# Banded attention in a hybrid layer kernel: the splitting and masking of a pair's probabilities issued in one group behind its turns

## The chip, the cores and the metric

The kernel runs on one core of a Trainium2 chip. The metric is the device time of one execution in microseconds. Five engines with queues of their own take part: TensorE (PE in the profile, with its weight loads as PEld), VectorE (DVE), ScalarE (ACT), GpSimd (POOL) and SyncE (SP, which here only issues DMAs). Each engine works its queue strictly in the order in which the program was written, and semaphores make an instruction wait for another engine.

## The reference

One decoder layer over 2048 positions and 1024 channels. A normalised and modulated input goes through one projection into two groups of heads: 8 heads of forgetting attention, and 8 query heads (2 key heads) of attention in a sliding window of 128 with sinks. Both outputs are gated, concatenated and projected back. What the change touches is the window attention:

```python
s = einsum('bnqhgd,bnshd->bnhgqs', qb, kk) * d ** -0.5     # a block of 128 queries, its own and the previous 128 keys
mask = (rel >= 0) & (rel < WINDOW) & valid_blk              # the band
s = where(mask, s, -inf)
p = softmax(concatenate([s, sink], -1), -1)[..., :-1]       # the sink is one more column of the softmax
out = einsum('bnhgqs,bnshd->bnqhgd', p, vv)
```

## The kernel before

**The window attention is done in 32 pairs.** A `Pair` is two neighbouring blocks of 128 queries for two heads, so four 128x128 tiles. Its steps, with the engine and the line:

- `scores` (PE, L871): 12 products in 16-bit halves into the PSUM tile `pss`, of which there is one.
- `maxima` (DVE): L879 folds the band of the previous key block into the own one, so that each row keeps 128 columns; L881 writes the sink into one more column; L884 takes the maxima; L886 makes the bias `b_nb` of 4 numbers a row from them.
- `exps` (ACT, L893): four exponentials of 128x129 into `sm_`, with their sums.
- `turn` (PE, L900): four transposes of `sm_` into the PSUM tile `pxb`. Then its two parts, which are not issued on the spot but registered with `after`: the **high part** (ACT, L914) rounds `pxb` to 16 bits into `fold[:, 0]`; the **low part** (DVE, L905) subtracts that from `pxb` into `fold[:, 1]`; a reciprocal of the sums (DVE, L907); and four **selections** on POOL (L909 and L911 for the high part, then both again for the low part), which write the two triangles of the band into `ptb`, zero elsewhere.
- `pv` (PE, L924): 24 products (18 for the first block) of `ptb` with the values into `pob`, and DVE's L930, which scales by the reciprocal into `on`. Two of eight pairs store `on` from the POOL queue at once (L274), the others after being split in two (L284, L280, L281).

`fold`, `ptb`, `sm_`, `pss` and `pxb` have one buffer each.

**Between these steps stand the projections.** `punits` is a list of units of TensorE work (3 products of 512 columns at L339, or 12 of 128 at L357), which make the queries, values and gates that are needed later. Their results leave PSUM through ACT and DVE (L731, L736, L383, L379, L362, L366), through three banks. Loading and splitting the projections' weights hangs on the same list: ACT's L256 makes the high part of a weight, DVE's L262 the low part, and POOL issues their loads (L216) and the small DMAs L225 and L230.

**What sets the order.** The order is written out by hand. `after(n, f)` puts `f` on a list, and `tick()` runs what is due. One round of the loop over the pairs is: `tick`, the maxima of the pair, a quarter of the units, `tick`, its exponentials, a quarter, `tick`, a quarter, `tick`, a quarter, then `pv` of the pair before, `turn` of this pair, `scores` of the next. So what a turn registers with `after(1, ...)` is issued at the head of the next round, in front of the next pair's maxima; what it registers with `after(2, ...)` is issued a quarter of a round later, behind the next pair's maxima and in front of its exponentials.

Of the kernel before, what the change touches and what calls it, by code (L numbers as in the profile page):

```python
# [15 lines left out]
AF = mybir.ActivationFunctionType  # L16
# [27 lines left out]
def hybrid_layer(  # L44
# [17 lines left out]
    V, A, G, PE, SP = nc.vector, nc.scalar, nc.gpsimd, nc.tensor, nc.sync  # L62
# [20 lines left out]
    def sm(n, tag):  # L83
        return small.tile([P, n], F32, tag=tag, name=tag)
# [112 lines left out]
    def after(n, f):  # L197
        late.append([n, f])
# [219 lines left out]
    def turn(ci, k):  # L418

        px = ps_x.tile([P, CH], F32, tag="x", name="px")  # L420
        for u in range(4):
            PE.transpose(px[:, u * P:(u + 1) * P], xt[ci * 4 + u][:, k * P:(k + 1) * P], ident[:])
        hf = hst.tile([P, CH], F32, tag="hf", name="hf")
        hi, lo = hT[ci][:, 0, k, :], hT[ci][:, 1, k, :]

        def scaled():
            for dst in ([hi] if k % 2 == 0 else []) + [hf[:]]:
                A.activation(dst, px[:], AF.Identity, scale=Gp[:, k:k + 1], bias=Shp[:, k:k + 1])

        def split():  # L430
            if k % 2:
                V.tensor_copy(hi, hf[:])
            V.tensor_tensor(lo, hf[:], hi, op=ALU.subtract)

        return scaled, split

    def turn_x(ci, k):
        scaled, split = turn(ci, k)
        after(1, scaled)
        after(2, split)  # L440
# [12 lines left out]
    with tc.manual_schedule():  # L453
# [172 lines left out]
        w_low("kb", 0, 1)  # L626
        w_low("vb", 0, 1)
        turned = [turn(0, k) for k in range(5)]
        squares(1)
        shf0 = col8("shf0")  # L630
# [22 lines left out]
        for k in range(KT):  # L653
            turned[k][0]()
            turned[k][1]()
            if k >= 2:
                next(root1, None)
            if k + 5 < KT:
                turned.append(turn(0, k + 5))
# [195 lines left out]
    class Pair:  # L855
# [40 lines left out]
        def turn(self):  # L896

            px = ps_t.tile([P, 4, P], F32, tag="t", name="pxb")
            for n in range(4):
                PE.transpose(px[:, n, :], self.sm_[:, n, 1:P + 1], ident[:])  # L900
            self.ptt = ptp.tile([P, 2, 2, 4, P], F16, tag="pt", name="ptb")
            fold = ptp.tile([P, 2, 4, P], F16, tag="fo", name="fold")

            def low():
                V.tensor_tensor(fold[:, 1], px[:], fold[:, 0], op=ALU.subtract)  # L905
                self.rinv = sm(4, "b_ri")
                V.reciprocal(self.rinv[:], self.rs[:])  # L907
                for n in range(2):
                    G.affine_select(self.ptt[:, 0, n], fold[:, n], [[0, 4], [-1, P]], ALU.is_ge, 0.0,  # L909
                                    base=-1, channel_multiplier=1)  # L910
                    G.affine_select(self.ptt[:, 1, n], fold[:, n], [[0, 4], [1, P]], ALU.is_ge, 0.0,  # L911
                                    base=0, channel_multiplier=-1)

            after(1, lambda: A.activation(fold[:, 0], px[:], AF.Copy))  # L914
            after(2, low)

        def pv(self):
            j, i = self.j, self.i
# [810 lines left out]
```

## Time and profile before

| | |
|---|---|
| median of 3 runs | 1174.29 us (1173.09 to 1176.38) |
| the profiled execution's own time | 1176.95 us |
| its span in the profile | 1175.2 us |
| DVE, ACT, POOL busy over the span | 80%, 56%, 16% |
| the pairs' part of the span | 149.0 us (first scores) to 431.1 us (last value products) |
| selections | 128, 91.4 us of POOL's 192.6 us |
| low parts | 32, 21.9 us of VectorE |

The rows of a timeline read: start in us, length in us, engine, line, operation, output and inputs by the program's names, partitions and size, count; in brackets the time for which the engine stood idle before, and the instruction on another engine that ended the wait. A group's row has the count, the busy sum and the mean in ns of one, and then the idle time before its instructions with those who ended it.

### The profile page before, as it was taken

The page shows a single profiled execution, that of the slowest core. Times are in us where ns is not written, and L with a number is a line of the kernel's source. Part 1 is how long each engine was busy: PE and PEld are TensorE (multiplying, and loading weights), DVE is VectorE, ACT ScalarE, POOL GpSimd, SP SyncE. Part 2 cuts the span into 40 slices and gives each one's busy share as a digit, 9 for nine tenths or more (in the row PEclk, how much of TensorE's full clock was granted, in tenths as well). Part 3 has the DMA queues.
Part 4 walks back from the last instruction along what each step waited for, and adds up shares of the span by engine and source line. Part 5 has one row for each costly group of instructions (what it writes and reads, how often), then busy time and mean ns, then how long its engine had stood idle before and what let it go on. Part 6 is the DMA issues. An engine that isn't in the chain of part 4 may idle for free.

```text
span 1175.2 us, 26821 instructions
## 1 busy us (share of the span) xinstructions
PE 1127.3 (96%) x10637; PEld 671.1 (57%) x10637; DVE 935.1 (80%) x2167; ACT 662.0 (56%) x1150; POOL 192.6 (16%) x293
## 2 busy tenths in 40 slices
PE   5899999999899999999999999999999999999997
PEld 2465555755457986555555555555556555544444
DVE  7876668688786757788888999888897897778885
ACT  2784445454554531476766767666776788543332
POOL 1000135535445531001000100001000000000000
PEclk9899999999999999999999999999999999999999
DMA  9745433414324323513425422223311237586743
GB/s 332 280 124 87 78 93 73 91 51 106 90 65 89 73 43 75 81 47 95 74 66 60 111 43 74 61 44 73 52 33 47 68 86 231 137 213 199 195 144 108
DMA packets 123481, 120.19 MB, mean 102 GB/s; under 512 B 64948, under 2 KB 100828, under 8 KB 123356
## 3 DMA queue, kind: packets, MB, share of 16 engines
q1 hardware_dynamic: 112088, 85.69, 27.0%
q0 software_dynamic: 10832, 32.50, 13.8%
q8 instruction: 83, 1.36, 0.6%
q14 instruction: 42, 0.34, 0.1%
q10 hardware_dynamic: 436, 0.28, 0.1%
HBM read 64.75 MB, written 25.18 MB: 77 GB/s over the span
## 4 chain that ended last, share of the span: by engine, by line
PE 71%; DVE 11%; issue 8%; DMA 5%; ACT 2%; POOL 2%; SPq 0%; DVEq 0%; ACTq 0%; POOLq 0%
PE bk L339 24%; PE bk L1522 13%; PE bk L357 7%; PE sta L1311 4%; PE sta L1310 4%; PE bk L1261 4%; PE poa L1336 3%; PE poa L1337 3%; PE poa L1334 3%; DMA wa<-in_w_ada_dram 2%; PE pob L924 2%; PE pss L871 1%; DVE a_m L1264 1%; DVE pha L1324 1%; PE pxb L900 1%
## 5 line engine op out<-in xcount | busy, mean ns | idle before, releaser
L1317 ACT ACTIVATE p<-sta,lift,scl_qk 128x1024 f32<-128x1024 f32 (+2 forms) x160 | 171.8, 1074 | 131.8 <-PE sta L1311 82.7
L339 PE MATMUL bk<-hT,wh_qk 128*128 128x512 f16 x768 | 194.7, 378 | 0.0
L1324 DVE TENSOR_TENSOR pha<-p,pha 128x1024 f16<-128x1024 f32 (+2 forms) x160 | 169.0, 1056 | 0.2 <-ACT pha L1321 0.2
L1264 DVE TENSOR_REDUCE a_m<-bk 128x1 f32<-128x512 f32 x192 | 130.3, 685 | 46.8 <-PE bk L1261 45.8
L1522 PE MATMUL bk<-wohl,oz 128*128 128x512 f16 x744 | 165.3, 379 | 1.0 <-DVE oz L1471 0.7
L1321 ACT ACTIVATE pha<-p 128x1024 f16<-128x1024 f32 (+2 forms) x160 | 148.1, 926 | 5.9 <-PE poa L1337 1.2
L1522 PEld LDWEIGHTS <-oz 128*128 128x128 f16 x744 | 71.8, 99 | 82.8 <-DVE oz L1471 1.8
L1337 PE MATMUL poa<-vt,pha 128*128 128x65 f16 x1088 | 116.1, 192 | 1.4 <-DVE pha L1324 1.4
L1334 PE MATMUL poa<-vt,pha 128*128 128x65 f16 x1088 | 116.6, 193 | 0.8 <-DVE ona L1343 0.7
L1336 PE MATMUL poa<-vt,pha 128*128 128x64 f16 x1088 | 116.6, 194 | 0.0
L339 PEld LDWEIGHTS <-wh_qk 128*128 128x128 f16 x768 | 72.2, 97 | 74.4 <-issue 1.9
L1310 PE MATMUL sta<-T 128*128 128x512 f16 (+1 forms) x320 | 110.9, 346 | 2.8 <-ACT p L1317 2.7
L1261 PE MATMUL bk<-T 66*128 66x512 f16 (+2 forms) x320 | 109.7, 348 | 3.2 <-DVE a_m L1264 1.9
L1334 PEld LDWEIGHTS <-pha 128*128 128x128 f16 x1088 | 101.5, 96 | 15.5 <-DVE ona L1343 1.9
L1311 PE MATMUL sta<-T 69*128 69x512 f16 (+1 forms) x320 | 109.8, 348 | 0.0
L1336 PEld LDWEIGHTS <-pha 128*128 128x128 f16 x1088 | 100.9, 97 | 11.4
L1337 PEld LDWEIGHTS <-pha 128*128 128x128 f16 x1088 | 100.8, 99 | 1.8 <-DVE pha L1324 1.8
L339 PE MATMUL bk<-hT,wh_za 128*128 128x512 f16 x384 | 99.7, 378 | 0.0
L357 PE MATMUL bk<-wh_va,hT 128*128 128x128 f16 x1536 | 89.9, 219 | 0.0
L357 PEld LDWEIGHTS <-hT 128*128 128x128 f16 x1536 | 87.1, 98 | 4.1 <-issue 2.1
L339 PE MATMUL bk<-hT,wh_zb 128*128 128x512 f16 x384 | 89.0, 380 | 0.0
L339 PE MATMUL bk<-hT,wh_qb 128*128 128x512 f16 x384 | 87.4, 379 | 0.0
(447 smaller groups left out, 1917.7 us busy)
## 6 DMA issues: line engine op xcount, KB each, us to landing
hT<-in_x_dram SPq DMA_DIRECT2D x20, 512.0 KB
wa<-in_w_ada_dram SPq DMA_DIRECT2D x16, 512.0 KB
z_d<-tz POOLq DMA_DIRECT2D x32, 256.0 KB, 3.0
T<-stq SPq DMA_DIRECT2D x64, 128.0 KB
T<-z_d SPq DMA_DIRECT2D x16, 512.0 KB
out_dram<-hT SPq DMA_DIRECT2D x15, 512.0 KB
xt<-in_x_dram SPq DMA_DIRECT2D x12, 512.0 KB
qs<-qf SPq DMA_DIRECT2D x80, 64.0 KB
```

Of the source, the lines that this page charges most:

```text
L339: PE.matmul(ps, whl[:, a, k, :], hT[ci][:, b, k, :], start=(k == 0 and n == 0), stop=(k == KT - 1 and n == 2))
L357: PE.matmul(ps[:, u * P:(u + 1) * P], hT[ci][:, a, k, u * P:(u + 1) * P], whl[:, b, k, :], start=(k == 0 and n == 0), stop=(k == KT - 1 an ...
L1261: PE.matmul(mx[:, :w], T[0:XM, 0, i * P:(i + 1) * P], T[0:XM, 2, pc * CH:pc * CH + w], start=True, stop=True)
L1310: PE.matmul(self.st[:, o:o + w], T[:, 3, kb_], T[:, 1, qc], start=True, stop=False)
L1311: PE.matmul(self.st[:, o:o + w], T[0:XR, 2, kb_], T[0:XR, 0, qc], start=False, stop=not diag)
L1317: A.activation(self.p32[:, :self.w], self.st[:, :self.w], AF.Exp, scale=scl[f"qk{self.hd}"][:], bias=lift[:])
L1321: A.activation(self.ph[:, 0, :self.w], self.p32[:, :self.w], AF.Copy)
L1324: V.tensor_tensor(self.ph[:, 1, :self.w], self.p32[:, :self.w], self.ph[:, 0, :self.w], op=ALU.subtract)
L1334: PE.matmul(po[:, u, :], ph[:, 0, pq], vt[:, b, hd, 0:65], start=(self.first and n == 0 and u == 0), stop=False)
L1336: PE.matmul(po[:, u, 0:64], ph[:, 0, pq], vt[:, b, hd, 65:VW], start=False, stop=False)
L1337: PE.matmul(po[:, u, :], ph[:, 1, pq], vt[:, b, hd, 0:65], start=False, stop=(self.last and n == len(self.blocks) - 1))
L1522: PE.matmul(py, self.hl[:, i, k, :], w_slot(8 * j + k)[:, cc], start=(k == 0 and m_ == 0), stop=(k == KT - 1 and m_ == 2))
```

## The change

The low part, the reciprocal and the four selections are issued at the first tick behind the turn instead of the second, together with the high part:

```diff
-            def low():
+            def split():
+                A.activation(fold[:, 0], px[:], AF.Copy)
                 V.tensor_tensor(fold[:, 1], px[:], fold[:, 0], op=ALU.subtract)
                 self.rinv = sm(4, "b_ri")
                 V.reciprocal(self.rinv[:], self.rs[:])
...
                     G.affine_select(self.ptt[:, 1, n], fold[:, n], [[0, 4], [1, P]], ALU.is_ge, 0.0,
                                     base=0, channel_multiplier=-1)
 
-            after(1, lambda: A.activation(fold[:, 0], px[:], AF.Copy))
-            after(2, low)
+            after(1, split)
```

The instructions, their sizes and their counts stay as they are, and so does the order on PE, ACT and SP. Lines from L905 on move by one or more: the high part is L905 in the changed kernel, the low part L906, the reciprocal L908, the selections L910 and L912.

On VectorE, at the pair whose turns run at 200.4 us of the profile, the difference reads (rows with + are the changed kernel's; `fold` is the split pair, `pss` the next pair's scores):

```order
 L930 TENSOR_TENSOR on<-pob,b_ri 128x256
+L906 TENSOR_TENSOR fold<-pxb,fold 128x512
+L908 RECIPROCAL b_ri<-b_rs 128x4
 L879 COPY_PREDICATED pss<-dmask,pss 128x2x2x128
 L881 COPY pss<-snd_qb_1543 128x2x2
 L884 TENSOR_REDUCE b_m<-pss 128x4
 L886 TENSOR_SCALAR b_nb<-b_m,nscl_qb_1541 128x4
-L905 TENSOR_TENSOR fold<-pxb,fold 128x512
-L907 RECIPROCAL b_ri<-b_rs 128x4
 L740 TENSOR_TENSOR stb<-qc,stb 128x512
```

The low part and the reciprocal move from behind the maxima's four instructions to in front of them; where VectorE had work of a projection between the maxima and the low part, they move past that too.

On POOL, at the selections of the pair whose turns run at 165.7 us, the rows of the kernel before (`o_d` and `z_d` are DRAM tensors, `tz` a gate projection that VectorE finishes after the maxima):

```order
L274 DMA o_d_69<-on 128x2x128
L381 DMA z_d<-tz 128x512
L909 AFFINE_SELECT ptb<-fold 128x512
L911 AFFINE_SELECT ptb<-fold 128x512
L909 AFFINE_SELECT ptb<-fold 128x512
L911 AFFINE_SELECT ptb<-fold 128x512
L225 DMA mx_d_74<-w_mx 128x1
```

and those of the changed kernel:

```order
L274 DMA o_d_69<-on 128x2x128
L910 AFFINE_SELECT ptb<-fold 128x512
L912 AFFINE_SELECT ptb<-fold 128x512
L910 AFFINE_SELECT ptb<-fold 128x512
L912 AFFINE_SELECT ptb<-fold 128x512
L381 DMA z_d<-tz 128x512
L225 DMA mx_d_74<-w_mx 128x1
```

The four selections pass the store of a gate, and stay behind the store L274 of the pair before, which waits for L930. At most other pairs POOL's order is the same before and after, and only the wait of the third selection for the low part ends at another time.

## The prediction

> **What bounds the kernel now.** I read the page's busy times first, then the stretch of the pairs by stages, then TensorE's own waits in it, then single pairs in the timeline.
>
> ```profile
> PE 1127.3 (96%) x10637; PEld 671.1 (57%) x10637; DVE 935.1 (80%) x2167; ACT 662.0 (56%) x1150; POOL 192.6 (16%) x293
> ```
>
> TensorE is busy nearly throughout, so only its idle time and its clock are to be had. By stages over 145 to 435 us, one stage and the sum (columns: stretch, length, busy PE, PEld, DVE, ACT, POOL, granted clock, DMA):
>
> ```profile
> 285.00:315.00 30.00, 26.60 (x200) 14.01 (x199) 22.02 (x58) 14.63 (x44) 15.49 (x23) 0.94 0.34 80
> ...
> sum 290.00, PE 282.48 PEld 190.65 DVE 214.78 ACT 141.99 POOL 138.68; mean PE 28.25 PEld 19.07 DVE 21.48 ACT 14.20 POOL 13.87
> ```
>
> TensorE idles 290.00 - 282.48 = 7.5 us, 3.4 of them in one stage, the only one whose clock is not 1.00: 6% of 30 us, 1.8 us more. The groups say who ended the idle time:
>
> ```profile
> L909 POOL TENSOR_SCALAR_AFFINE_SELECT ptb<-fold 128x512 f16<-128x512 f16 x64 | 46.5, 726 | 86.0 <-DVE fold L905 56.0 <-ACT fold L914 29.9
> ...
> L924 PE MATMUL pob<-vb,ptb 128*128 128x64 f16 x744 | 29.4, 194 | 7.1 <-POOL ptb L909 3.5 <-POOL ptb L911 3.1 <-issue 0.4
> ...
> L879 DVE COPY_PREDICATED pss<-dmask,pss 128x512 f32<-128x512 int16 x32 | 22.2, 694 | 18.0 <-PE pss L871 17.0 <-ACT fold L914 0.9
> L905 DVE TENSOR_TENSOR fold<-pxb,fold 128x512 f16<-128x512 f32 x32 | 21.9, 683 | 0.0
> ...
> L886 DVE TENSOR_SCALAR b_nb<-b_m,nscl_qb 128x4 f32<-128x4 f32 x32 | 8.3, 259 | 1.1
> ```
>
> The value products wait 3.5 + 3.1 = 6.6 us for selections, and selections wait 56.0 us for the low part, which is what the change brings forward. VectorE stands 17.0 us for scores in front of the maxima: the place into which the low part goes.
>
> **The typical pair.** Here is one, from its high part to the next turns:
>
> ```profile
> 201.16 0.60 ACT L914 ACTIVATE fold<-pxb 128x512 f16<-128x512 f32 x1 [2.90 <-issue]
> 201.83 0.63 POOL L909 TENSOR_SCALAR_AFFINE_SELECT ptb<-fold 128x512 f16<-128x512 f16 x1 [2.07 <-ACT fold L914]
> 201.95 0.70 DVE L879 COPY_PREDICATED pss<-dmask,pss 128x512 f32<-128x512 int16 x1 [0.88 <-PE pss L871]
> 202.42 0.63 POOL L911 TENSOR_SCALAR_AFFINE_SELECT ptb<-fold 128x512 f16<-128x512 f16 x1
> 203.61 0.23 DVE L886 TENSOR_SCALAR b_nb<-b_m,nscl_qb 128x4 f32<-128x4 f32 x1
> 203.75 0.69 DVE L905 TENSOR_TENSOR fold<-pxb,fold 128x512 f16<-128x512 f32 x1
> 203.94 0.46 ACT L893 ACTIVATE sm__2542<-pss,b_nb,scl_qb 128x129 f32<-128x129 f32 x1 [0.71 <-DVE b_nb L886]
> 204.43 0.66 DVE L740 TENSOR_TENSOR stb<-qc,stb 128x512 f16<-128x512 f32 x1
> 204.50 1.09 POOL L909 TENSOR_SCALAR_AFFINE_SELECT ptb<-fold 128x512 f16<-128x512 f16 x1 [1.45 <-DVE fold L905]
> 205.26 0.46 ACT L893 ACTIVATE sm__2542<-pss,b_nb,scl_qb 128x129 f32<-128x129 f32 x1
> 208.49 0.63 PE L900 MATMUL pxb<-ident,sm__2542 128*128 128x128 f32 x4
> ```
>
> Low part and reciprocal cost VectorE 204.43 - 203.75 = 0.68 us. In the new place the low part can start at the high part's end, 201.8, so the maxima begin at about 202.5 instead of 201.95: 0.55 us later, up to 0.68 where VectorE did not stand idle. VectorE is then through with both at the same time as before. The third selection could start when the second ends, at 203.0 instead of 204.50. The exponentials shift by those 0.55 us and end at 205.72 + 0.55 = 206.3; the turns stand at 208.49, so 2.2 us of slack hide it. At such a pair the change costs and gains nothing; the cover is this slack, and without it each pair would lose 0.55 to 0.68 us.
>
> **Where the cover is thin, by one more effect.** Four selections now run in one piece. The trace has that already, where a store held all four back:
>
> ```profile
> 213.14 0.39 DVE L280 TENSOR_TENSOR oh<-on,oh 128x256 f16<-128x256 f32 x1
> ...
> 263.75 2.93 DVE L280 TENSOR_TENSOR oh<-on,oh 128x256 f16<-128x256 f32 x1
> 264.00 0.65 POOL L909 TENSOR_SCALAR_AFFINE_SELECT ptb<-fold 128x512 f16<-128x512 f16 x1
> ...
> 265.76 0.63 POOL L911 TENSOR_SCALAR_AFFINE_SELECT ptb<-fold 128x512 f16<-128x512 f16 x1
> ```
>
> The same operation takes 0.39 us alone and 2.93 beside four selections, 264.00 to 266.39, a run of 2.39 us. So VectorE operations on SBUF stand until the run is over. The bias L886 is one (0.70 us beside selections, below, against 0.23). In the typical pair the run would last from 201.83 to 204.2 and the bias would be due at 203.61 + 0.55 = 204.16: just behind it. Where POOL starts late, behind the store L274, the bias waits.
>
> The Trainium skill, "SBUF — State Buffer", section "Who interferes with whom", says that a VectorE instruction with two SBUF inputs, or a scalar operation in a two-port mode, and a GpSimd instruction exclude each other, the later one blocking for the whole instruction of the first. Read so, the bias would wait for one selection only, and the sum below would come to a gain of 1.8 us (A 1.0, B -0.2, C 0.8, D 0.2), 1172.5 us; the 2.93 us row differs, a whole run is waited for, and the measurement decides.
>
> The 6.6 us fall on three places, A, B and C, and a remainder D of 0.2. At each, I ask what holds the turns when the selections no longer do: the exponentials.
>
> *A*, turns at 184.72, where 1.7 us of the waits lie just before:
>
> ```profile
> 178.58 0.71 POOL L274 DMA_DIRECT2D o_d<-on  x1 [1.48 <-DVE on L930]
> 182.00 0.46 ACT L893 ACTIVATE sm__2176<-pss,b_nb,scl_qb 128x129 f32<-128x129 f32 x1
> 184.72 0.63 PE L900 MATMUL pxb<-ident,sm__2176 128*128 128x128 f32 x4
> ```
>
> The store ends at 179.3, the run at 181.7, then bias and 1.8 us of exponentials (203.94 to 205.72 above): 183.6 instead of 182.46. The turns gain 184.72 - 183.7 = 1.0 us at most, and nothing if the pair before has pushed VectorE's list in the same way by 1 us. I take 0.4.
>
> *B*, turns at 250.01 and 259.16, with 1.5 us of the waits:
>
> ```profile
> 245.09 0.73 POOL L274 DMA_DIRECT2D o_d<-on  x1 [4.28 <-DVE on L930]
> 246.37 0.23 DVE L886 TENSOR_SCALAR b_nb<-b_m,nscl_qb 128x4 f32<-128x4 f32 x1
> 248.03 0.46 ACT L893 ACTIVATE sm__3396<-pss,b_nb,scl_qb 128x129 f32<-128x129 f32 x1
> 249.65 1.42 DVE L262 SCALAR_TENSOR_TENSOR wh_zb<-wr_zb,w_sw,wh_zb 128x512 f16<-128x512 f32 x2 [2.38 <-ACT wh_zb L256]
> 250.01 0.64 PE L900 MATMUL pxb<-ident,sm__3396 128*128 128x128 f32 x4
> 257.44 0.46 ACT L893 ACTIVATE sm__3529<-pss,b_nb,scl_qb 128x129 f32<-128x129 f32 x1
> 259.16 0.63 PE L900 MATMUL pxb<-ident,sm__3529 128*128 128x128 f32 x4
> ```
>
> Here VectorE is late, the store too, and the run would end at 245.82 + 2.39 = 248.2: the bias comes 1.65 us later. On ScalarE the weight L256 is queued behind the exponentials, on VectorE L262 waits for it, and the next maxima stand behind L262. So the next exponentials end at 257.90 + 1.65 + 0.68 = 260.2, and their turns lose 1.1 us. If the run held nothing, it would be 257.90 + 2 x 0.68 = 259.3, a loss of 0.2, or a gain of 0.3 with VectorE's shorter operations. Nearest to the row of 2.93, I take -0.8.
>
> *C*, turns at 299.57 and 311.17, with 3.4 us of the waits:
>
> ```profile
> 298.41 0.46 ACT L893 ACTIVATE sm__4104<-pss,b_nb,scl_qb 128x129 f32<-128x129 f32 x1
> 299.57 0.63 PE L900 MATMUL pxb<-ident,sm__4104 128*128 128x128 f32 x4
> ...
> 305.39 0.71 POOL L274 DMA_DIRECT2D o_d<-on  x1 [3.17 <-DVE on L930]
> 306.67 0.70 DVE L886 TENSOR_SCALAR b_nb<-b_m,nscl_qb 128x4 f32<-128x4 f32 x1
> 308.79 0.46 ACT L893 ACTIVATE sm__4232<-pss,b_nb,scl_qb 128x129 f32<-128x129 f32 x1
> 309.24 0.26 PE L924 MATMUL pob<-vb,ptb 128*128 128x64 f16 x3 [2.19 <-POOL ptb L909]
> 311.17 1.09 PE L900 MATMUL pxb<-ident,sm__4232 128*128 128x128 f32 x4
> ```
>
> At 299.57 the exponentials end at 298.87 + 0.68 = 299.55: no gain. The shift is carried by the same chain through the weights, so the store ends at 306.8, the run at 309.2, the exponentials at 311.1: the turns stay at 311.2. If the run held nothing, 309.25 + 2 x 0.68 - 0.47 (the bias at its usual 0.23) = 310.1, a gain of 1.0. I take 0.
>
> **Sum.** A 0.4, B -0.8, C 0, D 0.2: -0.2 us of gain. From the profiled execution's 1176.95 us that is 1177.2; it ran 2.7 us above the median of 1174.29, so 1174.5 against the median. Ends: 0 - 1.1 - 0.1 + 0.2 = -1.0 and 1.0 + 0.3 + 1.0 + 0.2 = 2.5, and the clock stage worth 1.8 us can vanish or appear a second time: from a gain of 4.3 to a loss of 2.8, so 1170 to 1177. What else moves costs nothing: POOL's store of a gate passes behind 2.4 us of selections, and no TensorE wait in the groups above names a bank or a store.
>
> **Rivals.** *All waits go.* For it: the waits for selections are nearly all that TensorE waits for, and operations such as the 2.93 us one fall back to 0.39, which makes VectorE early at B and C. Against: the 0.7 us between exponentials and turns at 299.57. It needs the bias not to be held. It gives 6.6 us, with the clock 8.4: 1166 to 1168.
>
> *The maxima are held in every pair.* The reciprocal now stands beside the selections in front of the maxima, and no row has it there. If it, or another member, waits for the run's end, the maxima come up to 2.4 us late. The typical slack of 2.77 us covers that; 259.16 - 257.90 = 1.26, 0.70 and 311.17 - 309.25 = 1.93 do not: losses of 1.1, 1.7 and 0.5, 3.3 us, about as much again at their neighbours (estimate). It decides from a delay of 0.7 us on. 1179 us.
>
> *The thin places lose more.* B's 1.1 us carried through, and two more stages at half clock for idle TensorE at B and A (3.6 us): 1179 us.
>
> **Chances.** About 0.3% (3.5 us) is what can be told from no change. Forecast 0.48; all waits go 0.19; maxima held 0.18; thin places 0.15. So faster 0.19, same 0.48, slower 0.33. The range reaches from partly into the first rival to a little beyond the last two: 1168.5 to 1181.
>
> **What would show it.** In the profile after: waits of L924 for selections near zero, and in their place waits of the turns L900 for exponentials at B and C, 1 to 3 us in all; L886 at 0.23 us in most pairs and 0.7 to 1.6 where L274 runs late; the low part's reciprocal at its 0.17 us; the third selection starting at the second's end. A reciprocal or bias of over 1 us at most pairs makes me wrong on the slow side, turns that never wait on the fast side.

## The result, and the profile after

The changed kernel takes 1172.14 us in the median of 20 runs (1169.87 to 1175.74), the kernel before 1174.92 (1172.32 to 1176.38) in 20 beside it. The ratio is 0.998, with an interval of 0.9972 to 0.9988: 1.4 to 3.3 us faster. That is less than the 3.5 us called measurable from a few runs, but it is not nothing, and it is a gain where 0.2 us of loss against the shown median was forecast. The profiled execution took 1173.47 us, with a span of 1171.7 us against 1175.2.

The page's busy times after:

```profile
PE 1126.7 (96%) x10637; PEld 671.1 (57%) x10637; DVE 924.3 (79%) x2167; ACT 661.7 (56%) x1150; POOL 182.4 (16%) x293
```

VectorE is busy for 935.1 - 924.3 = 10.8 us less, with the same 2167 instructions. POOL is busy for 10.2 us less. The pairs' stages after (same columns as before the change):

```profile
285.00:315.00 30.00, 29.56 (x248) 15.82 (x248) 22.28 (x57) 17.49 (x54) 12.91 (x21) 1.00 0.30 78
...
375.00:405.00 30.00, 27.44 (x475) 26.01 (x473) 17.99 (x41) 13.98 (x48) 12.63 (x20) 0.94 0.32 62
...
sum 290.00, PE 284.66 PEld 191.87 DVE 203.72 ACT 142.37 POOL 130.78; mean PE 28.47 PEld 19.19 DVE 20.37 ACT 14.24 POOL 13.08
```

The stage that had 3.4 us of idle TensorE and the half clock (285 to 315 us) is healed: 29.56 busy, clock 1.00. Instead another stage, 375 to 405 us, has 2.6 us of idle time and the 0.94. TensorE's waits in 145 to 435 us, with total, number and longest in us:

```profile
PE bk L357 <- issue: 2.8, 2, 2.6
PE bk L339 <- DVE wh_qb L262: 0.7, 1, 0.7
PE pxb L900 <- ACT sm__3529 L893: 0.5, 1, 0.5
...
PE pob L924 <- POOL ptb L912: 0.3, 1, 0.3
```

Of 6.6 us of waits for selections 0.3 are left. At the top stands a wait that the kernel before did not have: 2.6 us in one piece in front of a projection's product, put down to "issue", which means that the profile shows nothing that TensorE waited for. Idle time is not the whole account, since a turn that waits between its four transposes counts as busy. TensorE's progress shows it all: the starts of the turns, counted from the first scores (149.01 us before, 148.11 after). At the turns of the 29th pair (394.41 and 386.73) the changed kernel leads by 6.8 us, at the last turns (419.28 and 416.49) by 1.9. So the change gained 6.8 us, most of it in the places where the prediction looked, and lost 4.9 in a place where it did not, most of it 2.8 us of idle time and 1.8 us of half clock.

The pair that the prediction showed, after:

```profile
199.59 0.69 DVE L906 TENSOR_TENSOR fold<-pxb,fold 128x512 f16<-128x512 f32 x1 [0.41 <-ACT fold L905]
199.63 0.63 POOL L910 TENSOR_SCALAR_AFFINE_SELECT ptb<-fold 128x512 f16<-128x512 f16 x1 [1.88 <-ACT fold L905]
...
201.19 0.69 DVE L884 TENSOR_REDUCE b_m<-pss 128x4 f32<-128x516 f32 x1
201.39 0.63 POOL L912 TENSOR_SCALAR_AFFINE_SELECT ptb<-fold 128x512 f16<-128x512 f16 x1
201.92 0.23 DVE L886 TENSOR_SCALAR b_nb<-b_m,nscl_qb 128x4 f32<-128x4 f32 x1
202.05 0.69 DVE L740 TENSOR_TENSOR stb<-qc,stb 128x512 f16<-128x512 f32 x1
```

The four selections run from 199.63 to 202.02, beside the low part and the maxima, which all read PSUM and take what they took before (0.69 us for L906 and L884). The products that read two SBUF tiles (L740) come behind the run. That is nearly the whole effect on VectorE, and the groups show it, before and then after:

```profile
L746 DVE TENSOR_TENSOR qs<-qs,sinT 128x512 f32<-128x512 f32 x16 | 17.0, 1061 | 0.1
L280 DVE TENSOR_TENSOR oh<-on,oh 128x256 f16<-128x256 f32 x24 | 14.0, 582 | 0.0
```

```profile
L746 DVE TENSOR_TENSOR qs<-qs,sinT 128x512 f32<-128x512 f32 x16 | 11.0, 686 | 0.1
L280 DVE TENSOR_TENSOR oh<-on,oh 128x256 f16<-128x256 f32 x24 | 10.0, 418 | 0.0
L886 DVE TENSOR_SCALAR b_nb<-b_m,nscl_qb 128x4 f32<-128x4 f32 x32 | 10.7, 336 | 1.1
```

6.0 us less for L746 and 4.0 for L280, and 2.8 for the products L740 and L747 together. The bias L886 pays 2.4 us more, since it now falls into the run where POOL started late. It does not wait for the run's end there:

```profile
303.23 0.64 POOL L910 TENSOR_SCALAR_AFFINE_SELECT ptb<-fold 128x512 f16<-128x512 f16 x1
303.28 0.62 DVE L886 TENSOR_SCALAR b_nb<-b_m,nscl_qb 128x4 f32<-128x4 f32 x1
```

This is the third selection of a run that ends at 304.45, and the bias is through at 303.90. At four pairs it takes 0.62 to 0.65 us, one selection, and at one 1.25 us, two.

Where the stall at 299 to 311 us came from can be read backwards in the kernel before. These rows were not shown yet:

```profile
279.17 0.55 POOL L381 DMA_DIRECT2D z_d<-tz  x1 [2.84 <-DVE tz L379]
279.48 3.19 DVE L746 TENSOR_TENSOR qs<-qs,sinT 128x512 f32<-128x512 f32 x1
281.48 0.63 POOL L911 TENSOR_SCALAR_AFFINE_SELECT ptb<-fold 128x512 f16<-128x512 f16 x1
283.64 1.21 DVE L222 TENSOR_REDUCE w_mx<-wr_qb 128x1 f32<-128x1024 f32 x1
285.15 0.54 POOL L225 DMA_DIRECT2D mx_d<-w_mx  x1 [0.36 <-DVE w_mx L222]
285.68 0.54 POOL L230 DMA_DIRECT2D mxr<-mx_d  x1
293.72 0.29 DVE L241 TENSOR_REDUCE w_mx<-mxr 128x1 f32<-128x128 f32 x1 [1.89 <-issue]
```

and after:

```profile
277.05 0.68 DVE L746 TENSOR_TENSOR qs<-qs,sinT 128x512 f32<-128x512 f32 x1
278.71 1.21 DVE L222 TENSOR_REDUCE w_mx<-wr_qb 128x1 f32<-128x1024 f32 x1
280.22 0.54 POOL L225 DMA_DIRECT2D mx_d<-w_mx  x1 [0.36 <-DVE w_mx L222]
288.99 0.29 DVE L241 TENSOR_REDUCE w_mx<-mxr 128x1 f32<-128x128 f32 x1 [0.27 <-DMA mxr<-mx_d]
...
294.36 0.46 ACT L893 ACTIVATE sm__4104<-pss,b_nb,scl_qb 128x129 f32<-128x129 f32 x1
296.53 0.63 PE L900 MATMUL pxb<-ident,sm__4104 128*128 128x128 f32 x4
```

At the 15th pair the four selections stood behind the store of a gate (L381) and held one sine product for 3.19 us instead of 0.69. The reduction of the next weight (L222) came 2.5 us later, and with it the small DMA L225 and, behind it on POOL, the DMA L230, which reads back the maximum of the weight before. The scale L241 of that weight needs what L230 brings. VectorE stood 1.89 us in front of it, and the maxima behind it were late. L241 starts 8.1 to 9.3 us after this L225 in twelve of the kernels here, however long after L230 (5.4 to 8.2 us), so it goes with the store issued ahead of the read; why it does, no row shows. In the changed kernel the selections pass that store, and the chain runs with 0.27 us of waiting: the exponentials end 1.7 us ahead of the turns (294.82 to 296.53) where it was 0.7.

### The profile page after: what moved, and what is told of

It is laid out like the page before. It is cut to its first block, busy times and chain, and to the rows that moved or that the text cites. A ratio compares the mean times of both kernels' runs of the same rounds, so it can differ in the third digit from the quotient of the medians.

```text
span 1171.7 us, 26770 instructions
## 1 busy us (share of the span) xinstructions
PE 1126.7 (96%) x10637; PEld 671.1 (57%) x10637; DVE 924.3 (79%) x2167; ACT 661.7 (56%) x1150; POOL 182.4 (16%) x293
## 4 chain that ended last, share of the span: by engine, by line
PE 74%; DVE 13%; DMA 7%; ACT 3%; issue 2%; SPq 1%; POOL 0%; DVEq 0%; ACTq 0%; POOLq 0%
PE bk L339 27%; PE bk L1522 13%; PE bk L357 7%; PE sta L1311 4%; PE sta L1310 4%; PE bk L1261 4%; PE poa L1336 3%; PE poa L1337 3%; PE poa L1334 3%; DMA wa<-in_w_ada_dram 2%; DVE a_m L1264 2%; PE pss L871 1%; PE pob L924 1%; DVE pha L1324 1%; PE pxb L900 1%
## 5 line engine op out<-in xcount | busy, mean ns | idle before, releaser
L357 PE MATMUL bk<-wh_va,hT 128*128 128x128 f16 x1536 | 91.9, 221 | 2.9 <-issue 2.8
L357 PEld LDWEIGHTS <-hT 128*128 128x128 f16 x1536 | 88.7, 99 | 7.4 <-issue 5.4
```

Source lines behind the costliest of these rows:

```text
L357: PE.matmul(ps[:, u * P:(u + 1) * P], hT[ci][:, a, k, u * P:(u + 1) * P], whl[:, b, k, :], start=(k == 0 and n == 0), stop=(k == KT - 1 an ...
```

## The experiments

These ran in three groups, each on a chip of its own, with the kernel before beside them: 1178.05 us beside the first four, 1178.58 beside the next four (late_load to pair14) and 1179.34 beside the last four. So ratios to it are what is compared. Where TensorE's progress is given, it is the start of the turns since the first scores, against the profile of the kernel before that is shown above. In kernels with added lines the line numbers behind the addition are shifted.

### again, dve_only, behind_max, nosel_after: which part of the order does it

**again** is the changed kernel as it is.

> The changed kernel once more. Theory 1 (VectorE set free): the four selections now run beside the maxima, whose operations read PSUM and are not held, so VectorE loses about 11 us less in the pairs' part (about 203 us busy over 290 us against 214.8), is earlier where the turns were tight, and TensorE's waits for selections stay under 0.5 us; 1172 us against 1175. In the first profile of the changed kernel TensorE also stood 2.6 us for nothing that the profile shows, in a stretch of the last pairs, with 1.8 us of half clock behind it. If that belongs to the change, this profile has it at the same place and the profiled execution is near 1173; if it is chance, it is gone or elsewhere, and the profiled execution is near 1168 to 1170. Theory 2 (the prediction's terms): a gain of 0.2 us, 1174.7.

1177.54 us, ratio 0.999 (0.9976 to 1.0004).

```profile
PE bk L357 <- issue: 4.8, 2, 2.9
...
```

The stand is there again, at the same place of the same pair, with a second one of 1.9 us behind it. It belongs to the change. By the interval, the change cannot be told here from no change at all. The other waits, 0.8, 0.5 and 0.3 us, are those of the first profile.

**dve_only**: VectorE's order of the changed kernel, POOL's of the kernel before.

```diff
                 V.reciprocal(self.rinv[:], self.rs[:])
+            def select():
                 for n in range(2):
...
             after(1, split)
+            after(2, select)
```

> Low part and reciprocal in front of the maxima as in the changed kernel, the four selections issued at the second tick, so that POOL's order is that of the kernel before. Theory 1a (the gain comes from VectorE's order alone): 1172, waits for selections under 0.5 us. Theory 1b (the nine places where the selections pass a DMA of POOL carry part of it): at these places the selections still start late, behind the store of a gate, and hold the sine product L746 for about 3.2 us as before; the value products wait again at about 299 to 311 us for 3 us, with the half clock: 1174 to 1175. Theory 2: 1174.7 to 1176.

1182.27 us, ratio 1.0034 (1.002 to 1.0048): slower than both kernels, which neither theory had. Its waits and its held product:

```profile
PE bk L357 <- issue: 4.2, 2, 3.1
PE pob L927 <- POOL ptb L912: 2.3, 3, 0.9
PE pob L927 <- POOL ptb L914: 1.8, 4, 0.8
```

```profile
279.22 0.69 DVE L746 TENSOR_TENSOR qs<-qs,sinT 128x512 f32<-128x512 f32 x1
279.94 3.17 DVE L747 TENSOR_TENSOR qc<-qc,qs 128x512 f32<-128x512 f32 x1
```

At the 15th pair the selections still stand behind the gate's store, and hold L747, the product behind L746, for 3.17 us. 4.1 of the 6.6 us of waits stay. The stand at the last pairs comes with the early low part alone, since POOL's order is the same there in all these kernels and only the end of the selections moves. So this kernel has the loss of the change (4.8 us of TensorE's progress from the 29th pair to the 30th) and little of its gain: it leads by 1.2 us at the 29th pair, and two stages have a clock of 0.94.

**behind_max**: POOL's order of the changed kernel, but low part and reciprocal directly behind the maxima.

```diff
-            after(1, split)
+            after(1, lambda: A.activation(fold[:, 0], px[:], AF.Copy))
+            self.split = split
...
                 wd.maxima()
+                windows[n - 1].split()
```

> POOL's order that of the changed kernel, but low part and reciprocal directly behind the maxima on VectorE. Theory 1a: the selections of the low part fall beside VectorE's products again as in the kernel before, VectorE's busy time comes back to 212 or more, the waits for selections to 3 us or more: 1174 to 1175. Theory 1b: the places where POOL's order decides are mended, the waits fall to 1 to 3 us: 1172 to 1174. Theory 2 (the low part in front delays the maxima and costs what it gains): 1174, no worse than the changed kernel.

1171.71 us, ratio 0.9937 (0.9919 to 0.9955): 6 us faster than the changed kernel beside it, which neither theory expected.

```profile
PE pob L924 <- POOL ptb L909: 1.8, 2, 1.4
PE pob L924 <- POOL ptb L911: 1.6, 3, 0.8
PE pob L924 <- issue: 1.4, 1, 1.4
```

It keeps 3.4 us of waits for selections, and has no stand of L357 (one of 1.4 us on the value products, at 375 us). No product is held for more than 1.14 us. The profile explains only a part of its time: this execution took 1174.42 us, the slowest of the six, its stage from 285 to 315 us still has a clock of 0.94, and TensorE gains 2.7 us in the pairs, 1.7 of them between the 16th and the 20th, where the changed kernel gains 4.5. So the early place of low part and reciprocal is not needed for a gain, and at the last pairs the loss comes with it. POOL's order alone brings a part of what is gained; how large a part, this profile does not show.

**nosel_after**: the changed kernel without selections; the value products read `fold`.

> The changed kernel without the four selections: the value products read the split pair itself, so the band's triangles are not cut out and the result lacks the mask. It shows what the selections still cost. Theory 1: nearly nothing is left to gain, as TensorE hardly waits for them and VectorE is held little (10.7 us of the bias against 7.4 unheld): 1171 to 1172, and VectorE's busy time in the pairs' part about 200 us. Rival: the selections still hold VectorE at the tight turns by 1 us or more each: 1168 to 1170.

1177.36 us, ratio 0.9988 (0.9974 to 1.0002), VectorE busy for 198.4 us of the 290, TensorE's waits for exponentials 0.2 us. It says little of what the selections still cost, since it has stands of L357 for 5.4 us in three places, and two stages at a clock of 0.94. Taking work off POOL moves POOL's loads too, and with them, it seems, the stands.

### late_load, before_early, to27: what the stand is

POOL issues two loads of 256 KB for the weights of a forgetting head (L216) right behind the selections of the 29th pair. Before:

```profile
399.76 1.81 POOL L216 DMA_DIRECT2D wr_qk<-in_w_in_dram  x2
```

```profile
395.74 6.20 PE L357 MATMUL bk<-wh_va,hT 128*128 128x128 f16 x108
```

After (POOL, then TensorE):

```profile
390.48 1.81 POOL L216 DMA_DIRECT2D wr_qk<-in_w_in_dram  x2
```

```profile
388.06 4.19 PE L357 MATMUL bk<-wh_va,hT 128*128 128x128 f16 x72
394.81 3.71 PE L357 MATMUL bk<-wh_va,hT 128*128 128x128 f16 x36 [2.56 <-issue]
```

In the kernel before, the loads are issued 4.0 us after these products begin; in the changed kernel, 2.4 us after: the selections end earlier, and the loads with them. The same 108 products that ran through in 6.20 us then stand for 2.56 us in the middle. The DMA rows of the changed kernel for 389 to 393.5 us, and for a like stretch without such loads, 375 to 379.5 us, show one packet each on the queue that loads instructions (0.02 MB; in the kernel before, eight of them from 144 to 240 us make 0.13 MB, so 16 KB each):

```profile
q8 instruction: 1, 0.02, 4.0%
```

```profile
q8 instruction: 1, 0.02, 1.4%
```

Of 16 engines in 4.5 us, 4.0% are 2.9 us and 1.4% are 1.0 us. The queue has such a packet about every 120 of TensorE's products with their weight loads (8 packets to 980 products in that stretch), so it is taken for TensorE's own instructions; no row says so. In the kernel before, the packet at that place takes 2.9 us too, without a stand; so its length alone is not the cause. Three kernels try the loads.

**late_load**: the changed kernel with these loads issued behind the next small DMA, L230.

```diff
+                if key == "qk0" and n == 0:
+                    lead = 37
                 if key == "zb0":
```

> The changed kernel with one load moved: the weight load of the first forgetting head (wr_qk, two DMAs of 256 KB, L216) that POOL issues right behind a run of selections at 390 to 393 us stands behind the next small DMA (L230) instead. In the changed kernel's profiles TensorE's own instruction load starts 0.2 to 0.4 us after its product number 3400 and the two weight loads are issued 1.3 us after it; TensorE then stands 2.6 to 3.1 us for nothing that the profile shows, and runs 3.4 us at half clock. In the kernel before the weight loads come 2.9 us after that product and TensorE does not stand. Theory A (the weight load, issued 1.6 us earlier because the selections end earlier, holds up the instruction load): that stand and the half clock of its stretch are gone, 3 to 5 us less than the changed kernel's 1177.5 beside a kernel before of 1178: 1172.5 to 1174.5. Theory B (the stand is TensorE running dry for another reason, such as its order or a bank): it stays, 1177.5.

1173.08 us, ratio 0.9951 (0.9936 to 0.9965), against 0.999 for the changed kernel in **again**: 4.6 us less.

```profile
395.72 0.22 PE L357 MATMUL bk<-wh_va,hT 128*128 128x128 f16 x1 [0.80 <-issue]
396.30 2.17 PE L357 MATMUL bk<-wh_va,hT 128*128 128x128 f16 x36 [0.36 <-issue]
```

```profile
375.00:405.00 30.00, 28.84 (x525) 27.24 (x523) 20.34 (x49) 14.96 (x51) 14.92 (x23) 1.00 0.28 66
```

The stand is 1.2 us instead of 2.9, the second one has gone, and so has the half clock. From the 29th pair's turns to the 30th TensorE loses 1.5 us, where it loses 4.7 in **again**. Here the loads are issued at 397.38 us, behind the stand, so what is left of it is not theirs.

**before_early**: the kernel before with the same loads in front of the pair's selections (the same two lines, with 46).

> The kernel before with that same load moved the other way, in front of the pair's selections, so that it is issued at or ahead of TensorE's instruction load. Theory A: TensorE stands 2 to 3 us there, where it does not in the kernel before, and a stretch runs at half clock: 2 to 5 us slower than before. Theory B: nothing changes, ratio 1.000.

1184.71 us, ratio 1.0048 (1.0031 to 1.0066), about 6 us slower.

```profile
407.39 2.79 PE L357 MATMUL bk<-wh_va,hT 128*128 128x128 f16 x25 [2.97 <-issue]
```

The kernel before gets a stand that it did not have, by the move of one load on another queue, ten us after the load is issued and one pair later than in the changed kernel. Its stage from 405 us on has a clock of 0.94, and the stand costs 4.4 us of TensorE's progress.

**to27**: the change in the first 28 pairs alone.

```diff
+            turned[0] += 1
+            if turned[0] <= 28:
+                after(1, split)
+            else:
+                after(1, lambda: A.activation(fold[:, 0], px[:], AF.Copy))
+                after(2, low)
```

> The change in the first 28 pairs alone, the last four in the old order. Theory A: the selections in front of that load end as late as before, the load keeps its distance to TensorE's instruction load, and the gain of the earlier pairs stays whole: as late_load, 1172 to 1174. Theory B: 1177.5.

1171.84 us, ratio 0.9945 (0.993 to 0.996): the whole gain and a stand of 1.0 us. The three times are about theory A's (before_early lost 6 us where it has 2 to 5), and theory B's are excluded. Two things do not fit: in before_early the stand comes a pair late, and in to27 the loads are issued 4.0 us into the products, as in the kernel before, and a stand of 1.0 us is there all the same. So the place of the loads decides over most of the loss, not all. How the loads keep TensorE waiting (in the DMA engines, at memory, in the queue's descriptors) no row shows, and it stays open; so does the 1 us that is left.

### pair14, nosel14, not14_late: where the gain is

**pair14**: the kernel before with the change at the 15th pair alone (`if turned[0] == 15` in the diff above).

> The kernel before with the change at one pair alone, the 15th, whose four selections before stood behind the store of a gate and ran in one piece beside the sine product L746 (3.19 us there against 0.69). Theory 1b: VectorE is 2.5 us earlier in that pair, the reduction L222 and the small DMA L225 behind it too, the scale L241 of the next weight no longer waits 1.9 us, the maxima of the pair after it are early, and the waits of 3.4 us with the half clock at 299 to 311 us are gone: 3 to 5 us faster than before. Theory 2 (the prediction's: the shift goes down the chain through the weights and nothing is gained there): 0 to 1 us.

1173.48 us, ratio 0.996 (0.9947 to 0.9974). One pair of 32 brings 4.7 us.

```profile
PE pob L934 <- POOL ptb L913: 2.8, 6, 0.8
PE pob L934 <- POOL ptb L911: 1.9, 3, 0.9
```

Of the 6.6 us of waits 4.7 are left, and there is no half clock in 285 to 315 us any more, 1.8 us. From the 16th pair's turns to the 20th TensorE gains 4.1 us, of the 4.5 of the whole change.

**nosel14**: the kernel before in its old order, without the four selections of that pair.

```diff
+                if windows.index(self) == 14:
+                    return
                 for n in range(2):
                     G.affine_select(self.ptt[:, 0, n], fold[:, n], [[0, 4], [-1, P]], ALU.is_ge, 0.0,
```

> The kernel before with every instruction in its old order, and without the four selections of one pair, the 15th (its value products read the split pair itself, so that this pair alone lacks the mask). It takes the suspected hold away with no change of order. Theory 1b: the sine product L746 takes 0.69 us there instead of 3.19, and what follows is what the change at that pair alone gave: the waits and the half clock at 299 to 311 us go, 4 to 5.5 us faster than before (ratio 0.996). Rival: the change at that pair helped because its low part or its small DMAs came earlier, not through the held product: 0 to 2 us.

1174.02 us, ratio 0.9962 (0.9951 to 0.9974), the same gain with no change of order, and the same 4.1 us from the 16th pair's turns to the 20th.

```profile
279.16 0.66 DVE L746 TENSOR_TENSOR qs<-qs,sinT 128x512 f32<-128x512 f32 x1
280.80 1.21 DVE L222 TENSOR_REDUCE w_mx<-wr_qb 128x1 f32<-128x1024 f32 x1
```

So the held product is the cause, and its 2.5 us go down the chain shown above to a stall 20 to 30 us later. POOL's lighter load is not: L225 waits for L222 here too (0.37 us), so L222 sets when it goes out.

**not14_late**: late_load with the old order at the 15th pair alone.

> The changed kernel with the moved weight load of late_load, and the old order at the 15th pair alone. Theory 1b (this pair carries most of the gain): L746 is held for about 3.2 us again, the products of the pairs 17 and 18 wait 2 to 3.5 us for selections with the half clock behind it, and the time is 3 to 5 us above late_load: 1176 to 1178 beside a kernel before of 1178.5. Rival (other pairs give as much): within 1.5 us of late_load, 1173 to 1174.5.

1176.96 us, ratio 0.998 (0.9968 to 0.9992), 0.0029 or 3.4 us above late_load, with L746 at 3.20 us and the value products waiting 1.7 us at 306 to 308 us, but at a full clock. By these ratios this pair carries a little more than half of late_load's gain of 5.8 us, and the other pairs 0.002 or 2.4 us; alone it gave 0.004, so the parts do not simply add. From the 16th pair's turns to the 20th TensorE gains 1.9 us here and 4.7 in late_load.

### hold, mix

**hold**: dve_only with the selections held until the next pair's bias is done.

```diff
             def select():
+                if latest[0] is not self:
+                    G.tensor_copy(sm(4, "b_hold")[:], latest[0].nb[:])
```

> The low part in front of the maxima, but all four selections held until the next pair's bias is done, by a small copy of it on POOL. Theory 1 (what the selections run beside decides): they fall beside VectorE's SBUF operations again, so VectorE's busy time in the pairs' part is 212 us or more against 203 to 206, the value products wait 3 us or more for selections, the weight load at the last pairs is late again and TensorE does not stand there: 1178 to 1182. Rival (the low part's early place is what counts): VectorE near 205, waits as in dve_only, 1177 to 1179.

1189.23 us, ratio 1.0091 (1.0075 to 1.0106), the waits for selections 12.1 us. The sum product L747 takes 19.4 us against 11.1 in the changed kernel, and VectorE 208.1 us in all: the hold is there, 4 us smaller than expected. The time is above what either theory gave: selections that start behind the bias also end later, and two stages have a clock of 0.94. There is no stand of L357, as theory A has it.

**mix**: the change in the first 18 pairs, behind_max's order from the 19th on.

> The likeliest best: the change in the first 18 pairs, and from the 19th on low part and reciprocal directly behind the maxima. The stall at 299 to 311 us should be gone as in the changed kernel, and the weight load at the last pairs should come 2.9 us behind TensorE's product 3400 as in behind_max, so that TensorE does not stand there. Theories 1b and A: 1168.5 to 1171, below behind_max's 1171.7 and late_load's 1173.1. If either is wrong, 1172 to 1175.

1172.67 us, ratio 0.9948 (0.9932 to 0.9964). In the pairs it is the best of all (TensorE busy for 286.7 of 290 us, clock 1.00), and yet not faster than behind_max or to27: TensorE has a new wait of 1.3 us at 839.7 us, long after the pairs, and late_load has one of 1.7 us just in front of 842.4 us. Both are put down to "issue", like the stand of L357, and what ends them stays open. behind_max, to27, mix and late_load all lie 0.005 to 0.006 under the kernel before, which is more than 5 us and 4.6 us or more better than the changed kernel's 0.999; their intervals overlap.

## Why the prediction was right or wrong

**The bound and the waits: right.** The waits for selections were what there was to gain, and they went from 6.6 to 0.3 us.

**"At such a pair the change costs and gains nothing": right for TensorE, wrong for the queues.** The typical pair moved as forecast: third selection at the second's end, maxima later by the low part, bias just behind the run at 0.23 us. But the selections' end moves too, and what POOL issues behind them.

**A, +0.4 taken, 0 to 1.0: right in kind.** 1.7 us of waits became 0.7, now for a weight's low part (L262). By the turns at 184.72 and 182.50 us the gain is 1.3, a little over the upper end, and 0.95 in **again**.

**B, -0.8 taken, -1.1 to +0.3: right in kind, too dark in size.** The waits for exponentials came as forecast. This turn begins 0.49 us late and takes 1.65 us instead of 0.63, because it waits for an exponential before each transpose:

```profile
255.87 1.65 PE L900 MATMUL pxb<-ident,sm__3529 128*128 128x128 f32 x4 [0.49 <-ACT sm__3529 L893]
```

So 1.5 us of waits for selections became 1.5 us for exponentials, and by the turns of the 14th pair (267.02 and 264.75) against those at A the gain is 0.0 us, in **again** too. What was wrong is the rule taken from the row of 2.93 us, that the bias stands until the run is over: at 244.70 it took 0.64 us, one selection, and nowhere more than 1.25 in this profile. The products with two SBUF inputs did wait for the whole run, the bias did not. The prediction's other sum, with the bias held for one selection (1172.5 us), is near the measured median, but by luck: it has 0.8 for C and nothing for the stand.

**C, 0 taken, -0.1 to +1.0: wrong, and the largest term.** 3.4 us of waits became 0.3, and the half clock of 1.8 us went; by the turns of the 16th and the 20th pair TensorE gains 4.5 us, in **again** 4.6. The failed step is the sentence "The shift is carried by the same chain through the weights". What the chain through the weights carried was a gain, the 2.5 us for which the sine product was held, 20 us earlier: taking that hold away alone gave 4.1 of the 4.5 us. The prediction had the row of a whole run held (2.93 us) and named, under the first rival, that such operations fall back to 0.39 us; it gave that rival 0.19 and kept it out of the terms at A, B and C, where, but for 0.5 us in B's upper end, VectorE was moved by the added 0.68 us only and not by what it no longer loses. Nor could the size be read off the row: the same hold at 333.33 us (L746, 3.20 us) had at most 0.3 us of TensorE's time behind it in the next 35 us.

**"What else moves costs nothing": wrong.** The order on POOL behind the selections was followed for waits of TensorE on stores and banks, not for what a load does to TensorE's own instruction stream. Cost: 2.6 us of standing and 1.8 us of half clock; by the turns, and with 0.6 us at the last pair, 4.9 us. No rival had this.

By the turns, A 1.3, B 0.0, C 4.5, 0.9 elsewhere in the pairs, less 4.9 for the last pairs: 1.9 us, against 2.8 us between the medians (the two profiled executions are 3.5 us apart, 0.9 of it ahead of the first scores). The prediction's -0.2 was close by luck: two missing terms of opposite sign nearly cancel. The first rival, "all waits go", is what happened at A and C; its 1166 to 1168 us failed by the stand. The maxima held in every pair did not occur: reciprocals took 0.17 us beside the selections.

The Trainium skill, "Runtime: NRT & Kernel Launch", section "Instruction fetch mechanics", says that each engine's instructions come in blocks of 16 KiB (256 instructions) over a DMA queue, at a cost that is mostly hidden. The trace agrees with the block (one 0.02 MB packet per 120 or so products and as many weight loads); if the stand is a wait for such a block, which no row shows, it is not hidden here: 4.6 us hang on where one pair of weight loads is issued (ratios 0.999 and 0.9951).

## What to carry to other kernels

When work on one engine can hold another, ask not only when it ends but what the other runs meanwhile: four selections in a run cost VectorE nothing beside operations that read PSUM, one or two selections' time at a small bias, and 2.5 us beside one product of two SBUF tiles, which came due as a TensorE stall 20 to 30 us later. Go through the whole list of rows that are far above their group's usual length before a term is set, and follow each to who waits behind it, small DMAs and their round trips included. And when a queue gets free earlier, look at the large loads behind it: in this kernel a load issued a microsecond or two sooner made TensorE stand in a dense run of small products. And count TensorE's gain by when it reaches the same instruction, not by its idle time alone.

## What was not expected of the hardware

TensorE stood 2.6 to 3.1 us for nothing that the profile names, with a stretch at half clock behind it that costs 1.8 us more, and whether it did hung for the most part on when a load on another queue was issued; the stand came up to ten us after the load. A move of that load by a few us was worth about 5 us either way (-4.6 on the changed kernel, +6 on the kernel before), as much as all the waits that the change was about.
